# Six raw weight buffers, the decay table moved, first quarters loaded at the release of their home, and another block order

## The chip, the cores and the metric

The kernel runs on one core of one Trainium2 chip. The metric is the device time of one execution in microseconds. The kernel before took 404.04 us, the median of three executions that lie between 403.84 and 404.21 us.

A core has a matrix engine (PE, with the loading of its stationary operand shown as PEld), a vector engine (DVE), an activation engine (ACT), a general engine (POOL) and an engine that here only issues transfers (SP). Each takes its own instructions strictly in the order in which the program lists them and waits on semaphores where it needs a result of another. Transfers are issued by SP and, where they add to what is already there, by POOL.

## The reference

A decoder layer in float32 on x of shape (1, 256, 1024):

```python
h = rms_norm(x, g_pre_mix[l])
proj = h @ w_in[l]
...
mo = merge_heads(moba_attention(mq, mk, split_heads(mv, MOBA_HEADS)))
...
ro = retention(rq, rk, split_heads(rv, RET_HEADS))
ro = ro * lax.rsqrt(jnp.mean(ro * ro, axis=-1, keepdims=True) + NORM_EPS)
ro = jax.nn.silu(rg) * merge_heads(ro).astype(x.dtype)
mix = jnp.concatenate([mo, ro], axis=-1) @ w_out[l]
x = x + rms_norm(mix, g_post_mix[l])
h = rms_norm(x, g_pre_cross[l])
mem_n = rms_norm(mem, g_mem[l])
c = cross_attention(h, mem_n, w_cq[l], w_ckv[l], w_co[l])
x = x + rms_norm(c, g_post_cross[l])
h = rms_norm(x, g_pre_ffn[l])
gu = h @ w_gate_up[l]
f = (jax.nn.silu(gu[..., :D_FF]) * gu[..., D_FF:]) @ w_down[l]
x = x + rms_norm(f, g_post_ffn[l])
```

D_FF is 2816. The retention multiplies its scores by a fixed table, `inner_decay`, which the kernel reads from its constants. The FFN holds about half of the weights, and the change is mainly about it.

## The kernel before

**Arithmetic.** A float32 operand is split in a high part and a low part: ACT copies it to a rounded type (line 193), DVE subtracts that copy from the original (line 194). A product is then three matmuls, high by high, high by low, low by high. All weights come in blocks of 128 x 1024 floats (512 KB), and each block goes the same way: SP loads it to a raw buffer, `split_weight` (line 177) splits it into a tile of 128 x 2 x 1024 from the ring `hl` of nine, and PE uses it.

**Buffers.** The pool `rawp` has `RAW` = 5 raw buffers. Three single tiles named `qv`, `kT` and `ret` (128 x 2048 floats each) hold attention operands at first and serve as "homes" in the FFN. The constants `cst` are one tile of 1600 columns, of which the last 1024 are the decay table (line 117), loaded by `mem_stats` (line 977) and read in `ret_scores` (line 425). The retention's values `rv` fill the first half of the tile `ret` (line 950).

**Steps.** The program is written out by a planner in Python. It makes a list of 259 steps, each some six or eight matmuls; the FFN begins with step 129. The loop over the steps (line 1034) issues the step's matmuls, then whatever side work has come due (`run_side`: evacuations, activations, transposes, whose delays in steps stand in the table `WAIT`), and then at most one split (lines 1145 to 1156). A split is issued when a ring tile will have been free for two steps, and either nothing else was issued in this step or its first use is near (`near`, `now`); `hold` forbids splits around the first steps of the FFN.

**Blocks of the FFN.** The first four of the 22 column tiles go as plain blocks (weights 64 to 71). The names in the lists mean: `r6` is the gate and the up block of column tile 6, taken in rows (four steps); `d3` is block 3 of the down projection (two steps, one for each half of the tokens); `2:5` is product 5 of column group 2 (two steps, one for each of two blocks a and b). The groups 2, 3 and 4 are computed as a fast 2 x 2 block product with seven products in place of eight. `USE` is the order in which PE takes the blocks, `SPLIT` the order in which they are split (and loaded).

**Chains.** Of the seven products of a group, number 2 has a weight block of its own. The weight of number 1 (W11) is loaded to the group's home `one`, that of number 3 (W22) to home `two`; these are the "first quarters". The weights of the others are sums that are made in the home: after a split, POOL issues a transfer that adds another quarter in place (line 202), or DVE adds the other home (line 200, groups 3 and 4). Home `one` serves products 1, 5, 6, 4 in this order, home `two` products 3 and 7. `HOMES` names them: group 2 has kT and qv, group 3 qv and kT, group 4 ret and qv.

**Loading.** `load_weight` (line 140) is called after every split of a plain block and takes the next entry of `queue`, so a block's load is issued after the split of the block five places earlier in the queue. A first quarter is an entry of the same queue: when it comes up, SP is given its load at once and then the next plain block's. SP takes these loads in order. A load to a raw buffer waits until the split that last read the buffer is done, and a load to a home until the last reader of the home is done.

**Evacuating a group.** `seven_done` (line 663): after product 2 DVE adds and ACT applies the SiLU `s_silu` steps later; after product 3 DVE subtracts and multiplies, and `s_t0` steps later PE transposes the first half of the tokens (`f_store`, line 651, the tile `c_f`); after product 4 ACT applies the SiLU (line 682), `s_mul` steps later DVE multiplies (line 684), and `s_t1` steps later PE transposes the second half. The first column tiles go through `ffn_gate` (SiLU, line 587, delay `fg0`) and `ffn_up` (product on DVE, line 578, transposes `f0_0` steps later, line 582).

Of the kernel before, what the change touches and what calls it, by code (L numbers as in the profile page):

```python
# [7 lines left out]
F32 = mybir.dt.float32  # L8
# [3 lines left out]
ALU = mybir.AluOpType  # L12
AX = mybir.AxisListType

P = 128
D = 1024
EPS = 1e-6
MOBA_HEADS = 8
RET_HEADS = 4
CROSS_HEADS = 4  # L20
RING = 9
RAW = 5
FFN_Q = 64
HOMES = {2: ('kT', 'qv', None), 3: ('qv', 'kT', None), 4: ('ret', 'qv', None)}
SEVEN = tuple(HOMES)
ON_CHIP = (3, 4)
USE = 'r6 r7 r4 2:1 r5 r20 d3 d0 r21 2:5 2:6 d2 d1 2:2 d21 2:3 d4 2:7 d5 2:4 3:1 d20 3:2 d8 d7 d9 d6 3:5 3:6 3:3 3:7 d11 3:4 4:1 d10 4:2 4:5 d13 d12 4:6 4:3 d14 4:7 d15 4:4'.split()
SPLIT = 'r6 r4 r7 r5 2:1 r20 d0 d3 r21 2:5 d2 2:2 2:3 2:6 d1 2:7 d21 d4 d5 2:4 3:1 3:2 d8 d7 d20 d6 d9 3:5 3:3 3:6 3:7 d11 4:1 3:4 d10 d13 d12 4:2 4:5 4:3 4:6 d14 4:7 d15 4:4'.split()
DOWN_END = (16, 17, 18, 19)
ROW_TILES = tuple(int(what[1:]) for what in USE if what[0] == "r")  # L30
ROWS_AT = FFN_Q + 8
# [2 lines left out]

WAIT = {
    "cpb0": 2, "cpb1": 1, "cpv0": 7, "cpv1": 1, "cu0": 3, "cu1": 4, "ex_c0": 2, "ex_c1": 1, "ex_m00": 0,
    "ex_m10": 0, "ex_m11": 4, "f0_0": 9, "f0_1": 7, "g_add": 0, "g_silu": 5, "gate0": 3, "gate1": 6,
    "gp1": 5, "gp2": 0, "k_add": 0, "k_hl": 3, "lag": 2, "low": 6, "mq": 0, "mrow": 3, "ms": 21, "mst": 5,
# [5 lines left out]
}  # L44
WARM = 9

# [6 lines left out]
def tile_hybrid_layer(  # L53
# [45 lines left out]
    def accC(name):  # L99
        return psC.tile([P, 4, P], F32, tag="C", name=name)  # L100

    cst = cpool.tile([P, C_END], F32, tag="cst", name="cst")
    xg = cpool.tile([P, 288], F32, tag="xg", name="xg")
    gp = xg[:, 0:32].rearrange("p (g k) -> p g k", g=4)
    x_sb = cpool.tile([P, 2, D], F32, tag="x", name="x_sb")
# [8 lines left out]
    msin = cst[:, C_MSIN:C_MSIN + 32].rearrange("p (t d) -> p t d", t=2)  # L114
    rcos = cst[:, C_RCOS:C_RCOS + 128].rearrange("p (t d) -> p t d", t=2)
    rsin = cst[:, C_RSIN:C_RSIN + 128].rearrange("p (t d) -> p t d", t=2)
    decay = cst[:, C_DEC:C_DEC + 1024].rearrange("p (h i) -> p h i", h=RET_HEADS)

    T = {}
    rstd = {}  # L120
# [16 lines left out]
    queue = []  # L137
    sums = {}

    def load_weight():  # L140

        if not queue:
            return
        q = queue.pop(0)
        kind, w = items[q][:2]
        if kind == "w":
            raws[q] = rawp.tile([P, D], F32, tag="raw", name=f"raw{q}")
            nc.sync.dma_start(raws[q], weights[w])
        else:
            g, home, part = items[q][2:5]  # L150
            if part == 0:
                sums[(g, home)] = actp.tile([P, 2, D], F32, tag=home, name=f"sum_{home}{g}")
            nc.sync.dma_start(sums[(g, home)][:, part, :], weights[w])
            if (g, home, part) in beside:
                home, w = beside[(g, home, part)]
                if part == 0:
                    sums[(g, home)] = actp.tile([P, 2, D], F32, tag=home, name=f"sum_{home}{g}")
                nc.sync.dma_start(sums[(g, home)][:, part, :], weights[w])
            load_weight()

    homes = {}
# [1 line left out]
    split_at = {}  # L163
    ret_kept = [1000, 1000]
    beside = {}

    def free_home(q, i):

        if len(ringed) < RING or last_use[ringed[-RING]] + WAIT["lag"] <= i:
            return "hl"  # L170
        if q >= FFN_Q and ("oT", 7, 1) in emitted:
            for tag in ("qv", "kT", "ret") if q < FFN_Q + 8 else ("ret",) if not ret_kept[0] - 8 < q <= ret_kept[1] else ():
                if tag not in homes or last_use[homes[tag]] + WAIT["lag"] <= i:
                    return tag
        return None

    def split_weight(q, parts=1, home="hl"):
        kind = items[q][0]
        if kind == "w":
            raw = raws.pop(q)  # L180
        else:
            g, tag, part = items[q][2:5]
            raw = sums[(g, tag)][:, part, :]
        if home == "hl":
            ringed.append(q)
            h = hlp.tile([P, 2, D], F32R, tag="hl", name=f"hl{q}")
        else:
            homes[home] = q
            h = actp.tile([P, 2, D], F32R, tag=home, name=f"hl{q}")
        w = D // parts  # L190
        for i in range(parts):
            n = slice(i * w, (i + 1) * w)
            nc.scalar.activation(h[:, 0, n], raw[:, n], AF.Copy)  # L193
            nc.vector.tensor_tensor(out=h[:, 1, n], in0=raw[:, n], in1=h[:, 0, n].bitcast(F32), op=ALU.subtract)  # L194
        hls[q] = h
        split_at[q] = step_no[0]
        if kind != "w":
            plus, more = items[q][5:7]
            if plus is not None:
                nc.vector.tensor_tensor(out=raw, in0=raw, in1=sums[(g, plus)][:, part, :], op=ALU.add)  # L200
            if more is not None:
                nc.gpsimd.dma_start(raw, weights[more], accum_op=ALU.add)
        if kind == "w":
            load_weight()

# [203 lines left out]
    def ret_scores():  # L409

        need("rqk0", "rqk1")
        for kb in range(2):
# [7 lines left out]
            for e in range(2):  # L420
                if kb == 0 or e == 0:
                    buf = tmp2k(f"ra{kb}{e}")
                a = buf[:, kb * e * 256:kb * e * 256 + 2 * n].rearrange("p (j i) -> p j i", j=2)
                T[f"ra{kb}{e}"] = a
                nc.vector.tensor_tensor(out=a, in0=s[e][:, 0:2 * n].rearrange("p (j i) -> p j i", j=2),
                                        in1=decay.rearrange("p (j e) i -> p e j i", e=2)[:, e, :, 0:n], op=ALU.mult)
            if kb == 0:
                yield WAIT["rs"]

# [233 lines left out]
    def seven_done(g, m, acc):  # L663
# [3 lines left out]
        elif m == 2:  # L667
            f = parts[(g, 1)]
            nc.vector.tensor_tensor(out=f, in0=acc, in1=f, op=ALU.add)
            yield WAIT["s_silu"]  # L670
            nc.scalar.activation(f, f, AF.Silu)
        elif m == 3:
            f = parts[(g, 6)]
            nc.vector.tensor_tensor(out=f, in0=acc, in1=f, op=ALU.subtract)
            nc.vector.tensor_tensor(out=f, in0=f, in1=parts[(g, 1)], op=ALU.mult)
# [239 lines left out]
    if kept:  # L915
        ret_kept[:] = kept[0], kept[-1]

    last_use, first_use = {}, {}
    for i, s in enumerate(steps):
        last_use[s[1]] = i  # L920
# [26 lines left out]
    T["kT"] = kr[:, 0:1024].rearrange("p (j m) -> p j m", j=4)  # L947
    T["rqT"] = kr[:, 1024:1536].rearrange("p (j m) -> p j m", j=2)
    T["rkT"] = kr[:, 1536:2048].rearrange("p (j m) -> p j m", j=2)
    T["rv"] = actp.tile([P, 2048], F32, tag="ret", name="rv")[:, 0:1024].rearrange("p (t d) -> p t d", t=2)  # L950
    st_tile("xT", "stA")
    st_tile("mixT", "stB")
    xr = [p4.tile([P, 4, 256], F32, tag="p4", name=f"xr{i}") for i in range(2)]
# [17 lines left out]
    def mem_stats():  # L971
        mn = []
        for t in range(2):
            m = pt4.tile([P, D], F32, tag="pt4", name=f"memn{t}")
            nc.sync.dma_start(m, mem[tok(t), :])
            mn.append(m)
        nc.sync.dma_start(cst[:, C_DEC:], consts[:, C_DEC:])
        spawn(load_gpost(0))
        yield WAIT["mst"]
        for t in range(2):  # L980
# [287 lines left out]
```

## Time and profile before

| what | us |
|---|---|
| median of three executions | 404.04 |
| the profiled execution | 404.05 |
| its span, first to last instruction | 402.2 |
| PE busy in the span | 392.8 |
| DVE busy | 298.5 |
| ACT busy | 253.0 |
| POOL busy | 28.8 |
| splits on DVE from a raw buffer (line 194), 114 of 1192 ns on average | 133.6 |
| the same on ACT (line 193), 114 of 1034 ns on average | 114.6 |

The span is counted from the first to the last instruction of the program; the profiled execution took 1.85 us more than its span. A busy PE is not a PE at its peak, since the ends of matmuls are modelled. Where PE lost time is therefore read from the starts of successive matmuls. The transfers move 83.50 MB at a mean of 208 GB/s; 110 loads of 512 KB go to raw buffers, at a median of 4.6 us from issue to landing, and 20 transfers of 512 KB add to a home, at a median between 6.0 and 6.7 us by home.

### The profile page before, as it was taken

What the parts mean: (1) busy time and instruction counts of PE and PEld (TensorE: products, weight loads), DVE (VectorE), ACT (ScalarE), POOL (GpSimd) and SP (SyncE); (2) the same over time, 40 slices, a digit from 0 to 9 for tenths busy, and PEclk for the clock granted to TensorE, in tenths of its full rate; (3) what the DMA queues carried; (4) which work ended last, traced back from release to release, by engine and by line L of the source; (5) the groups of instructions that cost most, each with busy time, mean ns of one, the idle gap of its engine ahead of it and who ended that gap; (6) DMA issues with size and microseconds to landing.
All of it is one profiled execution on the core that took longest, in us unless ns stands there. A gap on an engine that the chain in (4) does not pass through costs nothing.

```text
span 402.2 us, 5538 instructions
## 1 busy us (share of the span) xinstructions
PE 392.8 (98%) x2005; PEld 327.9 (82%) x2005; DVE 298.5 (74%) x436; ACT 253.0 (63%) x434; POOL 28.8 (7%) x41
## 2 busy tenths in 40 slices
PE   9999999999999999999999999999999899999993
PEld 5887777888888888988888888888888688888782
DVE  4875976685879977586667698887759594985964
ACT  5785973955767856485546956766756546664731
POOL 0010010200011000000010001001201020103000
PEclk9999999999999999999999999999999999999998
DMA  7997745268537575516274577989995979977402
GB/s 275 411 344 237 281 157 209 104 209 275 176 145 244 181 230 177 197 50 212 59 257 156 158 260 229 241 277 222 172 363 108 384 225 191 222 295 143 121 0 104
DMA packets 23787, 83.50 MB, mean 208 GB/s; under 512 B 2640, under 2 KB 2896, under 8 KB 23760
## 3 DMA queue, kind: packets, MB, share of 16 engines
q1 hardware_dynamic: 20736, 72.41, 51.4%
q0 software_dynamic: 2880, 10.49, 15.0%
q8 instruction: 15, 0.25, 0.3%
q10 hardware_dynamic: 144, 0.26, 0.2%
q14 instruction: 12, 0.10, 0.1%
HBM read 82.10 MB, written 1.05 MB: 207 GB/s over the span
## 4 chain that ended last, share of the span: by engine, by line
PE 87%; DVE 3%; issue 3%; DMA 3%; ACT 2%; POOL 1%; DVEq 0%; POOLq 0%; ACTq 0%
PE acc L1098 13%; PE acc L1074 11%; PE acc L1075 11%; PE acc L1076 11%; PE acc L1101 7%; PE x L1134 6%; PE down L1120 4%; PE down L1119 4%; PE down L1121 4%; PE y L1134 4%; PE acc L1062 3%; DMA raw<-in_weights_dram 3%; PE z L1134 2%; DVE hl L194 2%; ACT hl L193 1%
## 5 line engine op out<-in xcount | busy, mean ns | idle before, releaser
L194 DVE TENSOR_TENSOR hl<-raw,hl 128x1024 fp32r<-128x1024 f32 (+1 forms) x114 | 133.6, 1192 | 30.6 <-ACT hl L193 30.4
L193 ACT ACTIVATE hl<-raw 128x1024 fp32r<-128x1024 f32 (+1 forms) x114 | 114.6, 1034 | 3.2 <-DMA raw<-in_weights_dram 3.1
L1074 PE MATMUL acc<-hl,xT 128*128 128x512 f32 x80 | 32.9, 411 | 0.0
L1119 PE MATMUL down<-hl,fT 128*128 128x512 f32 x80 | 31.4, 393 | 0.0
L1076 PE MATMUL acc<-hl,xT 128*128 128x512 f32 x80 | 31.3, 392 | 0.0
L1120 PE MATMUL down<-hl,fT 128*128 128x512 f32 x80 | 31.3, 391 | 0.0
L1075 PE MATMUL acc<-hl,xT 128*128 128x512 f32 x80 | 31.2, 390 | 0.0
L1121 PE MATMUL down<-hl,fT 128*128 128x512 f32 x80 | 31.2, 390 | 0.0
L1098 PE MATMUL acc<-x2T,hl 128*128 128x512 f32 x96 | 23.9, 393 | 0.0
L194 DVE TENSOR_TENSOR hl<-sum_qv,hl 128x1024 fp32r<-128x1024 f32 x16 | 19.3, 1219 | 2.0 <-ACT hl L193 2.0
L1098 PEld LDWEIGHTS acc<-x2T,hl 128*128 128x128 f32 x96 | 17.5, 188 | 3.3
L194 DVE TENSOR_TENSOR hl<-sum_kT,hl 128x1024 fp32r<-128x1024 f32 x12 | 14.5, 1218 | 5.9 <-ACT hl L193 5.9
L1120 PEld LDWEIGHTS down<-hl,fT 128*128 128x128 f32 x80 | 15.0, 188 | 3.4 <-DVE hl L194 0.4
L1076 PEld LDWEIGHTS acc<-hl,xT 128*128 128x128 f32 x80 | 15.0, 188 | 3.3
L1074 PEld LDWEIGHTS acc<-hl,xT 128*128 128x128 f32 x80 | 15.1, 189 | 3.2 <-issue 0.3
L1121 PEld LDWEIGHTS down<-hl,fT 128*128 128x128 f32 x80 | 15.0, 188 | 3.2
L1134 PE MATMUL x<-hl,comb 128*128 128x512 f32 x72 | 17.6, 392 | 0.0
L1119 PEld LDWEIGHTS down<-hl,fT 128*128 128x128 f32 x80 | 15.0, 188 | 3.1
L1134 PE MATMUL y<-hl,comb 128*128 128x512 f32 x72 | 17.3, 389 | 0.0
L1075 PEld LDWEIGHTS acc<-hl,xT 128*128 128x128 f32 x80 | 15.1, 189 | 2.6
L1134 PE MATMUL x<-hl,x2T 128*128 128x512 f32 x72 | 17.0, 389 | 0.0
L193 ACT ACTIVATE hl<-sum_kT 128x1024 fp32r<-128x1024 f32 x12 | 12.5, 1053 | 6.1 <-DMA sum_kT<-in_weights_dram 4.7
(256 smaller groups left out, 867.2 us busy)
## 6 DMA issues: line engine op xcount, KB each, us to landing
raw<-in_weights_dram SPq DMA_DIRECT2D x110, 512.0 KB, 4.6
sum_kT<-in_weights_dram POOLq DMA_DIRECT2D x8, 512.0 KB, 6.2
sum_qv<-in_weights_dram POOLq DMA_DIRECT2D x8, 512.0 KB, 6.0
sum_qv<-in_weights_dram SPq DMA_DIRECT2D x6, 512.0 KB, 5.0
sum_kT<-in_weights_dram SPq DMA_DIRECT2D x4, 512.0 KB, 7.0
sum_ret<-in_weights_dram POOLq DMA_DIRECT2D x4, 512.0 KB, 6.7
gpost<-in_gpost_dram SPq DMA_DIRECT2D x3, 512.0 KB, 4.7
x_sb<-in_x_dram SPq DMA_DIRECT2D x2, 512.0 KB, 6.9
```

Of the source, the lines that this page charges most:

```text
L193: nc.scalar.activation(h[:, 0, n], raw[:, n], AF.Copy)
L194: nc.vector.tensor_tensor(out=h[:, 1, n], in0=raw[:, n], in1=h[:, 0, n].bitcast(F32), op=ALU.subtract)
L1062: nc.tensor.matmul(accs[(c, t)], T["xT"][:, hx, q, tok(t)], h[:, hw, :], start=begin, stop=False)
L1074: nc.tensor.matmul(acc, xh, h[:, 0, kk, :], start=(first and kk == 0), stop=False)
L1075: nc.tensor.matmul(acc, xh, h[:, 1, kk, :], start=False, stop=False)
L1076: nc.tensor.matmul(acc, xl, h[:, 0, kk, :], start=False, stop=(last and kk == 1))
L1098: nc.tensor.matmul(acc, hls[q][:, 0, k * P:(k + 1) * P], T[f"{st}_k"][:, k, :], start=begin, stop=end, skip_group_check=True)
L1101: nc.tensor.matmul(acc[:, 0:256], hls[q][:, 1, k * P:(k + 1) * P], T[st][:, 0, k, :], start=begin, stop=end, skip_group_check=True)
L1119: nc.tensor.matmul(acc, fh, wh, start=first, stop=False, skip_group_check=True)
L1120: nc.tensor.matmul(acc, fh, wl, start=False, stop=False, skip_group_check=True)
L1121: nc.tensor.matmul(acc, fl, wh, start=False, stop=last, skip_group_check=True)
L1134: nc.tensor.matmul(acc, a, h[:, w, kk, :], start=begin and kk == 0 and n == 0, stop=end and n == 2, skip_group_check=True)
```

## The change

There are six raw buffers in place of five. The decay table leaves the constants' tile and goes to the unused second half of the tile that holds the retention's values, which gives back the 4096 bytes of each partition that the sixth buffer takes. Group 4 has kT in place of qv as its home `two`. The first quarters of a group whose home served an earlier group are no longer taken from the queue of loads; SP is given their load right after the split of the last item that reads the home (`released`). The lists `USE` and `SPLIT` are in another order, and 11 delays of `WAIT` differ (`ret` only names an 8 that stood in the code). The work of each engine is otherwise the same: the same matmuls, splits and transfers.

```diff
-RAW = 5
+RAW = 6
 FFN_Q = 64
-HOMES = {2: ('kT', 'qv', None), 3: ('qv', 'kT', None), 4: ('ret', 'qv', None)}
+HOMES = {2: ('kT', 'qv', None), 3: ('qv', 'kT', None), 4: ('ret', 'kT', None)}
 SEVEN = tuple(HOMES)
 ON_CHIP = (3, 4)
-USE = 'r6 r7 r4 2:1 r5 r20 d3 d0 r21 2:5 2:6 d2 d1 2:2 d21 2:3 d4 2:7 d5 2:4 3:1 d20 3:2 d8 d7 d9 d6 3:5 3:6 3:3 3:7 d11 3:4 4:1 d10 4:2 4:5 d13 d12 4:6 4:3 d14 4:7 d15 4:4'.split()
-SPLIT = 'r6 r4 r7 r5 2:1 r20 d0 d3 r21 2:5 d2 2:2 2:3 2:6 d1 2:7 d21 d4 d5 2:4 3:1 3:2 d8 d7 d20 d6 d9 3:5 3:3 3:6 3:7 d11 4:1 3:4 d10 d13 d12 4:2 4:5 4:3 4:6 d14 4:7 d15 4:4'.split()
+HOME_LOADS = "late-sp"
+USE = 'r7 r6 r4 r5 2:1 r20 d0 r21 d3 2:5 2:6 d2 2:2 2:3 d1 d21 2:7 d4 2:4 d5 d20 3:1 d8 3:2 d9 d6 3:5 d7 3:6 3:3 3:7 d11 3:4 4:1 d10 d12 d13 4:5 4:2 4:6 4:3 d14 4:7 d15 4:4'.split()
+SPLIT = 'r6 r4 r7 r5 2:1 d0 r20 r21 2:5 d3 d2 2:2 2:3 2:6 d1 2:7 d21 2:4 d4 d5 3:1 3:2 d20 d8 3:5 d9 d7 d6 3:3 3:6 3:7 d11 4:1 3:4 d12 d10 4:2 d13 4:5 4:3 4:6 d14 4:7 d15 4:4'.split()
...
-    "ex_m10": 0, "ex_m11": 4, "f0_0": 9, "f0_1": 7, "g_add": 0, "g_silu": 5, "gate0": 3, "gate1": 6,
-    "gp1": 5, "gp2": 0, "k_add": 0, "k_hl": 3, "lag": 2, "low": 6, "mq": 0, "mrow": 3, "ms": 21, "mst": 5,
+    "ex_m10": 0, "ex_m11": 4, "f0_0": 3, "f0_1": 7, "g_add": 0, "g_silu": 4, "gate0": 3, "gate1": 6,
+    "gp1": 5, "gp2": 0, "k_add": 0, "k_hl": 3, "lag": 2, "ret": 8, "low": 6, "mq": 0, "mrow": 3, "ms": 21, "mst": 5,
...
-    "sc_c0": 0, "sc_c1": 0, "u0": 4, "u1": 3, "u2": 2, "u_add": 0, "u_mul": 4, "u_hl": 4, "xa_cross0": 0, "xa_cross1": 1,
-    "xa_mix0": 8, "xa_mix1": 4, "near": 12, "now": 4, "sum": 6, "ts": 3, "ts0": 3, "ts1": 5, "s_silu": 4, "s_t0": 2, "s_mul": 2, "s_t1": 1, "xd": 3, "xh_cross0": 1, "xh_cross1": 1, "xh_mix0": 2, "xh_mix1": 2, "xn0": 2, "xn1": 2, "hold0": 1, "hold": 2, "hold_low": 3,
-    "xs": 11, "fg0": 2, "fg1": 0, "xw_cross0": 4, "xw_cross1": 3, "xw_mix0": 4, "xw_mix1": 0,
+    "sc_c0": 0, "sc_c1": 0, "u0": 4, "u1": 3, "u2": 2, "u_add": 0, "u_mul": 2, "u_hl": 1, "xa_cross0": 0, "xa_cross1": 1,
+    "xa_mix0": 8, "xa_mix1": 4, "near": 14, "now": 4, "sum": 5, "ts": 2, "ts0": 3, "ts1": 4, "s_silu": 2, "s_t0": 2, "s_mul": 2, "s_t1": 1, "xd": 3, "xh_cross0": 1, "xh_cross1": 1, "xh_mix0": 2, "xh_mix1": 2, "xn0": 2, "xn1": 2, "hold0": 1, "hold": 3, "hold_low": 3,
+    "xs": 11, "fg0": 4, "fg1": 0, "xw_cross0": 4, "xw_cross1": 3, "xw_mix0": 4, "xw_mix1": 0,
...
-    cst = cpool.tile([P, C_END], F32, tag="cst", name="cst")
+    cst = cpool.tile([P, C_DEC], F32, tag="cst", name="cst")
...
+    def load_home(engine, g, home, part, w):
+
+        if part == 0:
+            sums[(g, home)] = actp.tile([P, 2, D], F32, tag=home, name=f"sum_{home}{g}")
+        engine.dma_start(sums[(g, home)][:, part, :], weights[w])
...
         else:
-            g, home, part = items[q][2:5]
-            if part == 0:
-                sums[(g, home)] = actp.tile([P, 2, D], F32, tag=home, name=f"sum_{home}{g}")
-            nc.sync.dma_start(sums[(g, home)][:, part, :], weights[w])
...
+            for key in firsts[q]:
+                if key[:2] not in follows:
+                    load_home(nc.sync, *key)
             load_weight()
...
             if more is not None:
                 nc.gpsimd.dma_start(raw, weights[more], accum_op=ALU.add)
+            for key in released.get(q, ()):
+                load_home(nc.gpsimd if HOME_LOADS == "late-pool" else nc.sync, *key)
...
-                                        in1=decay.rearrange("p (j e) i -> p e j i", e=2)[:, e, :, 0:n], op=ALU.mult)
+                                        in1=T["decay"].rearrange("p (j e) i -> p e j i", e=2)[:, e, :, 0:n], op=ALU.mult)
...
+    if HOME_LOADS != "early":
+        for home in ("kT", "qv", "ret"):
+            users = [key for key in loads if key[1] == home]
+            for a, b in zip(users, users[1:]):
+                follows[b] = a
+                released.setdefault(last_read[a], []).extend(sorted(loads[b], key=lambda k: k[2]))
...
-    T["rv"] = actp.tile([P, 2048], F32, tag="ret", name="rv")[:, 0:1024].rearrange("p (t d) -> p t d", t=2)
+    rvd = actp.tile([P, 2048], F32, tag="ret", name="rvd")
+    T["rv"] = rvd[:, 0:1024].rearrange("p (t d) -> p t d", t=2)
+    T["decay"] = rvd[:, 1024:2048].rearrange("p (h i) -> p h i", h=RET_HEADS)
...
-        nc.sync.dma_start(cst[:, C_DEC:], consts[:, C_DEC:])
+        nc.sync.dma_start(rvd[:, 1024:2048], consts[:, C_DEC:])
```

More of the change, by code (lines that the diff above doesn't have):

```diff
@@ L116, in tile_hybrid_layer @@
     rsin = cst[:, C_RSIN:C_RSIN + 128].rearrange("p (t d) -> p t d", t=2)
-    decay = cst[:, C_DEC:C_DEC + 1024].rearrange("p (h i) -> p h i", h=RET_HEADS)
     T = {}
@@ L149, in load_weight @@
         else:
-            g, home, part = items[q][2:5]
-            if part == 0:
-                sums[(g, home)] = actp.tile([P, 2, D], F32, tag=home, name=f"sum_{home}{g}")
[L153 to L158, printed above, removed]
+            for key in firsts[q]:
+                if key[:2] not in follows:
+                    load_home(nc.sync, *key)
             load_weight()
@@ L165, in tile_hybrid_layer @@
     beside = {}
+    firsts, follows, released = {}, {}, {}
     def free_home(q, i):
@@ L171, in free_home @@
         if q >= FFN_Q and ("oT", 7, 1) in emitted:
-            for tag in ("qv", "kT", "ret") if q < FFN_Q + 8 else ("ret",) if not ret_kept[0] - 8 < q <= ret_kept[1] else ():
+            for tag in ("qv", "kT", "ret") if q < FFN_Q + 8 else ("ret",) if not ret_kept[0] - WAIT["ret"] < q <= ret_kept[1] else ():
                 if tag not in homes or last_use[homes[tag]] + WAIT["lag"] <= i:
@@ L671, in seven_done @@
             nc.scalar.activation(f, f, AF.Silu)
+            emitted.add(("silu", g))
         elif m == 3:
+            need(("silu", g))
             f = parts[(g, 6)]
@@ L916, in tile_hybrid_layer @@
         ret_kept[:] = kept[0], kept[-1]
+    loads, last_read = {}, {}
+    for q, item in enumerate(items):
+        if item[0] == "w":
+            continue
+        kind, w, g, home, part, plus = item[:6]
+        if kind == "first":
+            firsts[q] = [(g, home, part, w)]
+            if (g, home, part) in beside:
+                firsts[q].append((g, beside[(g, home, part)][0], part, beside[(g, home, part)][1]))
+            for key in firsts[q]:
+                loads.setdefault(key[:2], []).append(key)
+        for h in (home, plus):
+            if h:
+                last_read[(g, h)] = q
+    if HOME_LOADS != "early":
[4 more added lines that the diff above has]
+                released.setdefault(last_read[a], []).extend(sorted(loads[b], key=lambda k: k[2]))
     last_use, first_use = {}, {}
```

## The prediction

> **What bounds the kernel now.** I read the page's busy table and its 40 slices first, then the busy time by stretch, then PE's waits, and then the chain of waits around the only hole.
>
> ```profile
> PE 392.8 (98%) x2005; PEld 327.9 (82%) x2005; DVE 298.5 (74%) x436; ACT 253.0 (63%) x434; POOL 28.8 (7%) x41
> ```
> ```profile
> PE   9999999999999999999999999999999899999993
> ```
> ```profile
> 250.00:310.00 60.00, 60.00 (x298) 50.87 (x297) 47.35 (x65) 39.86 (x59) 7.45 (x9) 1.00 0.87 228
> 310.00:320.00 10.00, 8.32 (x39) 6.66 (x39) 5.68 (x6) 3.83 (x6) 0.00 (x0) 1.00 1.01 353
> 320.00:370.00 50.00, 50.00 (x226) 41.39 (x225) 38.87 (x38) 28.43 (x34) 8.74 (x10) 1.00 0.84 222
> ```
>
> After start, stretch length and length again the columns are the busy time of PE, PEld, DVE, ACT and POOL, then PE's granted clock and the DMA share. PE is the bound: every slice but one reads 9 until the tail, and the one with 8 is at 310 to 320 us, where PE is busy for 8.32 of 10 us. The clock is 1.00 there. The change takes no matmul away, so it can only give back holes. PE's own waits say how many there are:
>
> ```profile
> PE c_f L654 <- DVE sg L684: 1.7, 1, 1.7
> PE warm L942 <- PEq L1258: 0.8, 1, 0.8
> ```
>
> The second longest is at the start, before the first weights. The first is the hole, and the chain of waits follows it back (start, duration, what):
>
> ```profile
> 306.81 1.23 DVE hl L194
> 308.04 0.02 issue
> 308.05 6.82 DMA raw<-in_weights_dram
> ...
> 314.95 1.07 ACT hl L193
> ...
> 316.05 1.23 DVE hl L194
> 317.27 0.61 DVE sg L684
> ```
>
> PE waits to transpose the second token half of group 2. Its product (line 684) stands on DVE behind the split of down block d6, whose raw weights landed only at 314.87, because SP could not issue the load before 308.05: the buffer was held until the split of 3:2a ended. SP's waits and issues confirm it:
>
> ```profile
> SPq L148 <- DVE hl L194: 11.5, 2, 10.2
> ```
> ```profile
> SPq L153 <- DMA sum_qv<-in_weights_dram: 12.5, 1, 12.5
> ```
>
> From 298 to 311 us SP stood 10.2 us at a raw buffer, and from 276 to 292 us 12.5 us at the home of 3:1's first quarters, with the raw loads queued behind.
>
> **What the hole costs.**
>
> ```profile
> 315.95 0.39 PE L1121 MATMUL down<-hl,f 128*128 128x512 f32 x1
> 318.02 0.63 PE L654 MATMUL c_f<-cst,sg 128*128 128x128 f32 x4 [1.68 <-DVE sg L684]
> ```
> ```profile
> 347.74 5.44 PE x L1134 x24
> ```
>
> Undisturbed matmuls start every 5.44 / 24 = 0.227 us, so one step of six is 1.36 us. The two starts above are 2.07 us apart: 2.07 - 0.23 = **1.84 us** lost. A second, small loss is at d14:
>
> ```profile
> 370.00 0.60 ACT L666 ACTIVATE s<-x 128x512 f32<-128x512 f32 x1 [5.15 <-PE x L1134]
> 370.50 1.05 ACT L193 ACTIVATE hl<-raw 128x1024 fp32r<-128x1024 f32 x1
> ```
> ```profile
> 372.53 0.39 PE L1119 MATMUL down<-hl,fT 128*128 128x512 f32 x1
> 372.86 0.50 PE L1120 MATMUL down<-hl,fT 128*128 128x512 f32 x1
> 373.20 0.40 PE L1121 MATMUL down<-hl,fT 128*128 128x512 f32 x1
> ```
>
> Starts 0.33 and 0.34 us apart in place of 0.227 lose 0.22 us: d14's split queued on ACT behind the evacuation of 4:6 (370.00).
>
> **The change part by part.** I walked the rules of lines 1143 to 1156 over the new lists and delays; that gives the step at which each split is issued. PE's steps keep their lengths, so times are counted in steps.
>
> *Six buffers.* One load per split is issued as before, five blocks ahead; what goes is the wait. A load takes the buffer of the block six places back, whose split is always an earlier one. In the new order the split between the SiLU and the product of group 2's second half is that of d8 (SiLU at step 194, d8 at 195, product at 196, transposes at 197). Its load stands on SP behind 3:3's two first quarters, which wait for the split of 2:4b:
>
> ```profile
> 300.93 0.69 DVE L674 TENSOR_TENSOR s<-y,s 128x512 f32<-128x512 f32 x1 [2.48 <-PE y L1134]
> 301.72 0.69 DVE L675 TENSOR_TENSOR s<-s,s 128x512 f32<-128x512 f32 x1
> 302.33 1.22 DVE L194 TENSOR_TENSOR hl<-sum_kT,hl 128x1024 fp32r<-128x1024 f32 x1
> ```
> ```profile
> DMA to landing us min/median/max: 3.4/4.6/10.4
> ```
> ```profile
> 261.27 0.90 SPq L153 DMA_DIRECT2D sum_qv<-in_weights_dram  x2
> ```
>
> PE ends 2:3b some 0.2 us before 300.93, the order on DVE stays, so 2:4b's split ends 2.8 us after 2:3b. Two issues on SP (0.90) bring d8's load to 4.0 us with its own, and a raw load lands 3.4 to 10.4 us later (the row is that of line 148): between 7.4 and 14.4 us. ACT wants it after the SiLU of 2:4, which ends ten steps later: 10 x 1.36, 0.44 of transposes, 0.2 and 0.6 make 14.8 us. Even the slowest load of the trace is in time. Without this cover each microsecond of lateness is one of PE.
>
> *The wait after the data.* SiLU, one split, product, transposes: the same sequence stands in group 3 of before, with the raw weights there in time.
>
> ```profile
> 350.49 0.60 ACT L682 ACTIVATE sg<-x 128x512 f32<-128x512 f32 x1 [1.10 <-PE x L1134]
> ```
> ```profile
> 353.21 0.68 DVE L684 TENSOR_TENSOR sg<-s,sg 128x512 f32<-128x512 f32 x1
> ```
> ```profile
> 354.38 0.60 PE L654 MATMUL c_f<-cst,sg 128*128 128x128 f32 x4
> ```
>
> The product ends at 353.89, the transposes start 0.5 us later without a wait. So the 1.84 us go, with a cover of some 0.5 us.
>
> *d14.* Its split is issued at step 235, ahead of the evacuation at step 236. It then starts at least 0.6 us earlier: 0.22 us go.
>
> *First quarters late.* 3:1's loads wait for 2:7b's split as before; what was queued behind them on SP is now ahead of them. 3:3's no longer wait for their turn in the queue, and 4:3's wait for 3:7b in home kT instead of 3:4b in qv, five steps earlier. Nothing on POOL is moved past a wait: its 20 accumulating transfers come in the order of the splits.
>
> *Decay table.* The same transfer at the same place; the tile's next user is the cross-attention's query, long after. Cost 0; the retention finds the table loaded.
>
> *Order and delays.* No split is issued fewer than four steps (5.4 us) before its use; in the old order d14 had three and 4:6b two. A split needs 1.05 on ACT and 1.23 on DVE, and up to 0.8 behind an evacuation: 3.1 us. The rest, 2.3 us, covers a second split in front (1.2). The tightest new place is the opening of the FFN, below. Before the FFN the order is unchanged and PE has no hole that loads could close, so earlier raw loads bring 0 there.
>
> **Sum.** 404.05 (profiled, span 402.2 and 1.85 around it) - 1.84 - 0.22 = 401.99; the median is 0.01 below the profiled execution, so **402.0 us**. Below it there is no other hole to close; 401.7 leaves room for the spread of the three executions. Above it stand the rivals.
>
> **Rivals.**
>
> *A new wait at the opening* (faster all the same). `f0_0` 9 to 3 asks for the first transposes six steps earlier, `fg0` 2 to 4 for the SiLU two steps later.
>
> ```profile
> 226.53 1.28 ACT L587 ACT_TABLE_LOAD   x1
> 227.83 0.60 ACT L587 ACTIVATE sg<-acc 128x512 f32<-128x512 f32 x1
> 228.32 1.14 ACT L511 ACTIVATE x2T<-xt_cross,xg 128x128 fp32r<-128x128 f32 x4
> ```
> ```profile
> 226.64 0.44 PE xt_cross L508 x4
> ```
>
> After the transposes end (227.08) the new order has on ACT a wait of 0.2, four evacuations (1.14), a split (1.05), the table load (1.28) and the SiLU (0.60), then the product on DVE (0.69, as DVE's operations of that size above): 4.9 us. PE comes to the transposes four steps later, 5.4 us: a cover of 0.5 us. If DVE takes one split (1.22) in front, PE loses 0.7: **402.7 us**.
>
> *The wait comes back elsewhere* (no change). The cover of 0.5 us before group 2's transposes is less than one split: a second one in front of the product on DVE costs 0.7, and data late by 1 us more costs the rest. That the sixth buffer doesn't help because five loads are issued ahead as before belongs here; SP's 10.2 us at the buffer speak against it, since the load's turn had come. **403.2 to 404.5 us.**
>
> *Accumulating transfers get slower* (slower). SP's loads now run further ahead, beside POOL's.
>
> ```profile
> DMA to landing us min/median/max: 5.4/6.1/10.5
> ```
> ```profile
> 328.31 0.88 POOL L202 DMA_DIRECT2D sum_kT<-in_weights_dram  x1 [20.25 <-DVE hl L194]
> ```
>
> The second row is that of line 202; the stretch with the hole has a DMA share of 1.01. The closest chain: 3:3a is split at step 205 and 3:7a, which needs its sum, used at 217: 16.3 us less one step (1.36) for step 205 itself is 15.0. The split behind an addition of group 3 takes 0.2 + 0.69 + 1.23, the issue 0.2 + 0.88, then the landing, and 3:7a's own split 2.3: 5.5 us and the landing, so 9.5 us of landing are covered. The median leaves 3.4 us, the slowest (10.5) costs 1.0. Slower than before by over 0.2% needs 2.06 + 0.81 = 2.9 us: landings near 12.4 us at one place, or 10.5 at three of the chains' pairs. Priced at 11.2 at each of two pairs: 2 x 1.7 = 3.4, **405.4 us**. Against it: the same number of bytes moves, and loads that start earlier are also done earlier.
>
> The Trainium skill ("DMA: Bandwidth & Descriptors", "Issuing engines are not separate DMA queues") says the same thing against the change: transfers started by different engines run on the same 16 DMA engines and interleave. The stretch's DMA share agrees that there is no room at such moments; by that rule this rival's time would come out, by the landings of the trace the forecast. The page's fit for a transfer ("Anatomy of one DMA", 2.0 us and the bytes over 436 GB/s) would give an estimate of 3.2 us for 512 KB and no such rival at all; the trace's median of 6.1 us is what decides.
>
> **How the numbers follow.** Chances: the forecast with up to 0.6 us of small new waits (401.7 to 402.6) 0.60; a new wait at the opening or like it (402.6 to 403.2) 0.10; the wait back elsewhere 0.17; slower 0.13. Some 0.2% (0.8 us) is what a measurement of this kernel can tell from no change, so faster means under 403.23, slower over 404.85: 0.70, 0.17, 0.13. The range takes in the first two and most of the third, 401.7 to 404.0.
>
> **What would show it.** Right: in the stretch of the second transposes of group 2 PE is busy throughout, the row of `c_f` behind `sg` is gone from PE's waits, SP no longer stands 10 us at a raw buffer there, and d14's matmuls start 0.227 us apart. Wrong: a wait of `c_f` behind `f` or `sg` (first and second rival), or of PE behind `hl` with ACT waiting for an accumulating transfer (third).

## The result and the profile after

The changed kernel took 401.37 us, the median of four executions between 401.11 and 401.58 us. The kernel before took 404.02 us in the same comparison (four executions, 403.84 to 404.21). The ratio is 0.9934, with a 95% interval from 0.9917 to 0.9951. The forecast was 402.0 us in a range from 401.7 to 404.0: the direction was right, and the time lies 0.33 us below the range's lower end. The profiled execution after took 401.58 us and its span is 399.8.

The page of the changed kernel, its busy times and PE's 40 slices:

```profile
PE 392.3 (98%) x2005; PEld 328.0 (82%) x2005; DVE 299.8 (75%) x436; ACT 254.3 (64%) x434; POOL 28.7 (7%) x41
...
PE   9999999999999999999999999999999999999993
```

The work is the same, 2005 matmuls among it, and the slice that read 8 now reads 9. The busy time by stretch, in the columns used before (start, length twice, PE, PEld, DVE, ACT, POOL, PE's clock, DMA share, GB/s):

```profile
250.00:310.00 60.00, 60.00 (x297) 50.83 (x297) 47.44 (x62) 39.09 (x58) 6.98 (x8) 1.00 0.90 242
310.00:320.00 10.00, 10.00 (x48) 8.29 (x47) 6.99 (x7) 6.47 (x8) 0.00 (x0) 1.00 0.99 340
320.00:370.00 50.00, 50.00 (x226) 41.37 (x226) 38.53 (x38) 29.49 (x35) 8.72 (x10) 1.00 0.81 207
```

In the middle row PE was busy for 8.32 us with 39 matmuls, now for 10.00 with 48. PE's waits in the whole execution (waited in total, times, longest) are down to two, and neither is in the FFN:

```profile
PE warm L968 <- PEq L1286: 0.8, 1, 0.8
PE c_R_mem L246 <- POOL r_mem L217: 0.2, 1, 0.2
```

The place of the old hole, in the timeline of PE and then of DVE (start, duration, what). The transposes of group 2's second half start 0.24 us after the last matmul ahead of them; it was 2.07 us.

```profile
313.01 0.40 PE L1149 MATMUL down<-hl,f 128*128 128x512 f32 x1
313.25 0.60 PE L657 MATMUL c_f<-cst,sg 128*128 128x128 f32 x4
```

```profile
310.94 1.23 DVE L195 TENSOR_TENSOR hl<-raw,hl 128x1024 fp32r<-128x1024 f32 x1 [1.79 <-ACT hl L194]
312.08 0.68 DVE L689 TENSOR_TENSOR sg<-s,sg 128x512 f32<-128x512 f32 x1
```

The product ends at 312.76, so the transposes have a cover of 0.5 us, as forecast. The split in front of it is now that of d8, whose load had been issued by 299.20 and landed at 304.16, 5.7 us before ACT took it at 309.85. SP's waits from 298 to 311 us:

```profile
SPq L154 <- DVE hl L195: 7.5, 4, 4.1
```

The longest wait at a raw buffer fell from 10.2 to 4.1 us. At d14 the matmuls start 0.23 and 0.22 us apart, which were 0.33 and 0.34:

```profile
370.44 0.39 PE L1147 MATMUL down<-hl,fT 128*128 128x512 f32 x1
370.67 0.39 PE L1148 MATMUL down<-hl,fT 128*128 128x512 f32 x1
370.89 0.39 PE L1149 MATMUL down<-hl,fT 128*128 128x512 f32 x1
```

**A measure that leaves the start out.** From here on the starts of the matmuls are used in two parts: "48th" is the start of the 48th matmul of the first weights (line 1062 before, 1090 after), and "rest" the time from there to the start of PE's last matmul. What remains of a profiled execution behind and around them is 8.75 us before and 8.64 after, and between 8.6 and 9.2 in all 14 profiles of this study.

| profile | 48th | rest | its time |
|---|---|---|---|
| before | 16.59 | 378.71 | 404.05 |
| after | 16.37 | 376.57 | 401.58 |

The rest fell by 2.14 us, where the forecast said 1.84 + 0.22 = 2.06. The profiled times differ by 2.47: 2.14, 0.22 by which this start came sooner, and 0.11 around.

### The profile page after: what moved, and what is told of

It reads as the page before. It is cut to its first block, busy times and chain, and to the rows that moved or that the text cites. A ratio compares the mean times of both kernels' runs of the same rounds, so it can differ in the third digit from the quotient of the medians.

```text
span 399.8 us, 5537 instructions
## 1 busy us (share of the span) xinstructions
PE 392.3 (98%) x2005; PEld 328.0 (82%) x2005; DVE 299.8 (75%) x436; ACT 254.3 (64%) x434; POOL 28.7 (7%) x41
## 4 chain that ended last, share of the span: by engine, by line
PE 92%; DVE 3%; issue 2%; ACT 1%; POOL 1%; DVEq 0%; POOLq 0%; ACTq 0%
PE acc L1126 13%; PE acc L1102 11%; PE acc L1103 11%; PE acc L1104 11%; PE x L1162 8%; PE acc L1129 7%; PE down L1147 5%; PE down L1149 4%; PE down L1148 4%; PE y L1162 4%; PE acc L1090 3%; PE z L1162 2%; PE warm L968 1%; DVE hl L195 1%; ACT p_m L310 1%
## 5 line engine op out<-in xcount | busy, mean ns | idle before, releaser
L195 DVE TENSOR_TENSOR hl<-sum_kT,hl 128x1024 fp32r<-128x1024 f32 x16 | 19.5, 1221 | 8.3 <-ACT hl L194 8.3
L194 ACT ACTIVATE hl<-sum_kT 128x1024 fp32r<-128x1024 f32 x16 | 16.7, 1053 | 2.3 <-DMA sum_kT<-in_weights_dram 2.3
L1126 PE MATMUL acc<-memT,hl 128*128 128x512 f32 x64 | 16.3, 396 | 0.0
```

What stands on the lines that cost most here:

```text
L1126: nc.tensor.matmul(acc, hls[q][:, 0, k * P:(k + 1) * P], T[f"{st}_k"][:, k, :], start=begin, stop=end, skip_group_check=True)
```

## The experiments

Two questions were open. Which part closes the hole: the sixth buffer, the new order, or the late first quarters? And why is the time lower than the sum allowed: is there a further gain (for one, that a sixth buffer lets SP load further ahead from the first weights on, so that PE starts sooner), or was the kernel before profiled in an execution that started late? All kernels were timed in five rounds, beside the kernel before on the same chip. That one had medians of 403.64 (14 executions), 403.36 (23) and 403.48 us (9) there, and lay anywhere from 402.87 to 405.02.

### The parts one by one

The changed kernel again, unedited:

> The changed kernel once more, unchanged, to size the gain with more rounds. Theory A (only the two holes of the FFN are closed, 1.84 + 0.22 us, and the rest of the measured 2.65 us is scatter of the executions): 2.0 to 2.2 us under the kernel before, ratio 0.9945 to 0.9950, and the first weight matmul starts as often near 4.99 us as near 4.89 us. Theory B (the sixth buffer or the new place of the tiles also starts the kernel sooner): 2.4 to 2.8 us under it, ratio 0.993 to 0.994, and the excess of the first ten microseconds stays near 1.08 us where before had 1.30 us.

Measured: 401.25 us (six executions, 400.76 to 401.69), ratio 0.9938 [0.9922, 0.9954]. The rest is 376.59, 0.02 from the first profile; the 48th matmul starts at 15.75, 0.62 us sooner. One kernel, two starts. By its time it lies where theory B put it, 2.39 us under the kernel before; by its rest, 2.12 us under that of before, it lies with theory A.

Buffers alone: six raw buffers and the table moved to make room, with the old order and the old way of loading (the diff is against the kernel after).

```diff
-HOMES = {2: ('kT', 'qv', None), 3: ('qv', 'kT', None), 4: ('ret', 'kT', None)}
+HOMES = {2: ('kT', 'qv', None), 3: ('qv', 'kT', None), 4: ('ret', 'qv', None)}
-HOME_LOADS = "late-sp"
+HOME_LOADS = "early"
...
-USE = 'r7 r6 r4 r5 2:1 r20 d0 r21 d3 ...
+USE = 'r6 r7 r4 2:1 r5 r20 d3 d0 r21 ...
...
```

> The kernel before with six raw buffers and the decay table in the retention's tile; old order, delays and homes, first quarters still taken from the queue. Theory A: the load of d6 is issued near 298 us in place of 308 us, the hole of 1.84 us at group 2's second transposes goes, the 0.22 us at d14 stay: 402.2 us, ratio 0.9955. Theory B: 0.3 to 0.6 us less, 401.6 to 401.9 us. Theory C (the order of the blocks is what closes the hole, and buffers don't): near 404.0 us, with the wait of c_f behind sg kept.

Measured: 401.92 us (401.40 to 402.70), 0.9955 [0.9939, 0.9972]; the rest is 376.88, that is 1.83 below before. PE's timeline at the old hole:

```profile
315.78 0.40 PE L1149 MATMUL down<-hl,f 128*128 128x512 f32 x1
316.02 0.60 PE L657 MATMUL c_f<-cst,sg 128*128 128x128 f32 x4
```

The hole is gone, since d6's load no longer waits for 3:2a's split: it landed at 304.41. The ratio is the one that theory A gave. The loss at d14 stays, 0.22 of the 0.31 us that it has more than the kernel after.

The order alone: five buffers and the old way of loading, with the new lists and delays.

```diff
-RAW = 6
+RAW = 5
...
-HOME_LOADS = "late-sp"
+HOME_LOADS = "early"
```

> The changed kernel with five raw buffers and the first quarters taken from the queue as before; new order, delays and homes, table moved. Theory A (as refined here: either a sixth buffer or the new order is enough, since in the new order the split in front of the product is that of d8, whose buffer d4 gives back near step 189, so that the load has some 5 steps before it is wanted): no wait of c_f, d14 closed too, 402.0 us, ratio 0.995. Theory C: the same 402.0 us. A theory in which the buffers alone do it: the hole of 1.84 us is still there, 403.8 us.

Measured: 401.44 us (nine executions, 400.88 to 403.11), 0.9950 [0.9933, 0.9966]; the rest is 377.15. This closes the hole too, but leaves a small new loss. SP's issues in its timeline (x4 are four loads), and PE's timeline 37 us later:

```profile
302.13 7.11 SPq L154 DMA_DIRECT2D raw<-in_weights_dram  x4
309.34 1.37 SPq L144 DMA_DIRECT2D sum_kT<-in_weights_dram  x2
```

```profile
346.33 0.39 PE L1149 MATMUL down<-hl,fT 128*128 128x512 f32 x1
346.80 0.70 PE L1162 MATMUL x<-hl,x2T 128*128 128x512 f32 x2
```

3:3's first quarters come only after loads that stand at raw buffers, so the sum of 3:7 is late; the two starts are 0.47 apart in place of 0.227, 0.24 us, and 0.19 more go at 343 us. In the kernel after SP issues these two loads at 297.92.

The late first quarters alone: five buffers, the old lists, delays and home, and `HOME_LOADS = "late-sp"`.

```diff
-RAW = 6
+RAW = 5
...
-USE = 'r7 r6 r4 r5 2:1 r20 d0 r21 d3 ...
+USE = 'r6 r7 r4 2:1 r5 r20 d3 d0 r21 ...
...
```

> The kernel before with the first quarters loaded at the release of their home, five raw buffers, old order, delays and homes, table moved. Theory A: d6 still waits for the buffer of 3:2a (issue near 308 us), its load lands 1 us sooner at best since fewer transfers are under way, and the hole keeps 0.8 to 1.84 us: 403.0 to 404.0 us. A rival, that SP blocked by 3:1's first quarters was the cause of the late load: hole gone, 402.2 us.

Measured: 406.45 us, the median of five executions between 405.57 and 407.24 (a sixth took 802.27, which nothing here explains, and is left out); 1.0067 [1.0047, 1.0086]: **slower than before**, which neither of the two forecasts had. The rest is 381.24, 2.53 us more than before. The chain of waits has the hole of before, with a slower load:

```profile
307.16 7.80 DMA raw<-in_weights_dram
...
315.04 1.07 ACT hl L194
...
316.13 1.23 DVE hl L195
317.36 0.61 DVE sg L689
```

This execution started 0.90 us sooner (its 48th at 15.69), so the load was issued at the same point of the work as in before (308.05 there). It took 7.80 us in place of 6.82, and PE's hole is 3.04 - 0.23 = 2.81 us in place of 1.84: the delay passes straight through. Then comes a second loss. PE's timeline, and the stretch by busy time:

```profile
315.06 0.39 PE L1149 MATMUL down<-hl,f 128*128 128x512 f32 x1
318.10 1.09 PE L657 MATMUL c_f<-cst,sg 128*128 128x128 f32 x4 [2.66 <-DVE sg L689]
...
319.41 0.63 PE L1148 MATMUL down<-hl,f 128*128 128x512 f32 x1
319.84 0.63 PE L1149 MATMUL down<-hl,f 128*128 128x512 f32 x1
```

```profile
318.00:321.00 3.00, 2.90 (x9) 2.54 (x10) 0.89 (x2) 1.77 (x3) 0.00 (x0) 0.50 1.03 414
```

Behind the hole the granted clock is 0.50 and the matmuls start 0.43 us apart in place of 0.227. The trace's record of the clock says half speed for 3.413 us, from 317.91 to 321.32. That is what remains, 2.53 - 0.97 = 1.56 us.

### The parts with one turned back

The change with five buffers:

```diff
-RAW = 6
+RAW = 5
```

> The changed kernel with five raw buffers in place of six. Theory A (each of the two, sixth buffer and new order, closes the hole by itself; late first quarters do no harm where the split in front of the product isn't late): no wait of c_f, PE needs 376.6 us from the 48th matmul of the first weights to its last one, as in the changed kernel, about 2.1 us under the kernel before (ratio 0.995) and what is left of the difference is the start. Rival (late first quarters with five buffers make the load late, as they did in the old order): a hole of 1 to 3 us near 313 us, 403 to 405 us.

Measured: 401.80 us (401.11 to 402.58), 0.9954 [0.9936, 0.9972]; the rest is 376.59.

The change with the old way of loading:

```diff
-HOME_LOADS = "late-sp"
+HOME_LOADS = "early"
```

> The changed kernel with the first quarters taken from the queue of loads again (six buffers, new order). Theory A: the hole stays closed; the 0.6 us that PE lost near 343 and 346 us with five buffers came from 3:3's quarters that were issued only at 309 us behind a raw buffer; with six they are issued some 4 us earlier: loss under 0.2 us, 376.6 to 376.8 us from the 48th matmul to the last, ratio 0.994 to 0.995. Rival (late loading is needed by the new order whatever the buffers): the 0.6 us stay, 377.2 us.

Measured: 401.79 us (400.72 to 402.39), 0.9950 [0.9931, 0.9968]; the rest is 376.61. In the new order either of the two is enough: PE's work behind the start is the same to 0.04 us with both, with the sixth buffer alone, and with the late loading alone.

The change with the old order (six buffers, late loading, old lists, delays and home):

```diff
-USE = 'r7 r6 r4 r5 2:1 r20 d0 r21 d3 ...
+USE = 'r6 r7 r4 2:1 r5 r20 d3 d0 r21 ...
...
```

> Six raw buffers and late first quarters in the old order with the old delays and homes. Theory A: d6 takes the buffer of d5, issued near 298 us, so the hole and the slow clock after it go; d14's 0.22 us stay: 376.85 us from the 48th matmul to the last, ratio 0.9955. Rival (the late quarters of 3:3 delay d6's load whatever the buffers): a hole of 1 us or more near 315 us.

Measured: 402.46 us (twelve executions, 401.69 to 403.44), 0.9970 [0.9957, 0.9982]; the rest is 378.58, as in before. The main expectation missed: in the profiled execution the hole is back, 1.70 us long.

```profile
314.97 0.39 PE L1149 MATMUL down<-hl,f 128*128 128x512 f32 x1
316.89 0.63 PE L657 MATMUL c_f<-cst,sg 128*128 128x128 f32 x4 [1.53 <-DVE sg L689]
```

SP's waits from 290 to 312 us, and the chain:

```profile
SPq L144 <- DVE hl L195: 11.0, 2, 9.0
```

```profile
301.35 1.23 DVE hl L195
...
302.60 0.33 SPq L144
...
302.98 0.42 SPq L144
...
303.44 10.30 DMA raw<-in_weights_dram
...
313.83 1.07 ACT hl L194
...
314.92 1.23 DVE hl L195
316.15 0.61 DVE sg L689
```

SP stands 9.0 us at line 144, the loads of 3:3's first quarters, until 2:4b's split at 301.35 is done. d6's raw load is queued behind them, is issued at 303.44 and takes 10.30 us, where the median of such loads in this trace is 5.1. A raw buffer was free. So two things make this hole: the place in SP's queue, which left 8.5 us until ACT wanted the block (its SiLU ends at 311.92), and a slow transfer. The forecast had priced this very wait for the new order, where 2:4b is split three steps earlier and the split behind the SiLU is d8's: there the load had 5.7 us to spare.

The profiled execution took 403.09 us and was the second slowest of the twelve. The earliest 48th matmul of the 14 profiles (15.60), this rest and the least that remains around it in any of them (8.64) make 402.82 us, and nine of the twelve executions were faster than that. In them the hole must have been shorter or absent, which fits a load whose landing decides.

The decay table alone: before, with the table moved.

```diff
-        nc.sync.dma_start(cst[:, C_DEC:], consts[:, C_DEC:])
+        nc.sync.dma_start(rvd[:, 1024:2048], consts[:, C_DEC:])
```

> The kernel before with only the decay table moved to the retention's tile. Theory A: no difference, 378.7 us from the 48th matmul to the last, hole of about 1.84 us, ratio 1.000 within 0.2%. Theory B (places in memory or six buffers start the kernel sooner): the 48th matmul comes earlier than the 16.59 us of the kernel before only in kernels with the new place; here then by 0.2 us or more and the time by as much under the kernel before.

Measured: 403.56 us (twelve executions, 402.98 to 404.93), 1.0004 [0.9992, 1.0016]; the rest is 378.59. It costs nothing. The 48th matmul starts at 15.85, 0.74 us sooner than in the profile of before, but the time isn't lower, and a start at 17.21 came with the new place too: nothing speaks for theory B.

All eight combinations of order, buffers and loading are now there; "order" stands for the lists, the delays and group 4's home together, which no run takes apart. The rest in us, of one profile each:

| | early, 5 buffers | early, 6 | late, 5 | late, 6 |
|---|---|---|---|---|
| old order | 378.71 | 376.88 | 381.24 | 378.58 |
| new order | 377.15 | 376.61 | 376.59 | 376.57 |

Two of these are not the rest of every execution: 378.58, as said above, and 377.15, since three of nine executions (400.88 to 401.21) lie under 15.60 + 377.15 + 8.64 = 401.39 us.

### The start

The 14 profiles start their 48th matmul between 15.60 and 17.21 us, at a median of 15.82. Of the ten up to here, with that of before and the first after, five have six buffers and a mean of 16.19 (16.37, 15.75, 16.38, 16.82, 15.62), and five have five buffers and a mean of 16.19 too (16.59, 17.21, 15.69, 15.60, 15.85). So these profiles show no sooner start with the sixth buffer; a few tenths of a microsecond could hide in their scatter. What varies is seen in the chains of the first 20 us: before, after, the change with five buffers, and the change with early loading, of which the first pieces of the start are left in.

```profile
4.99 11.99 PE acc L1062 x48
```

```profile
4.89 11.86 PE acc L1090 x48
```

```profile
4.75 11.24 PE acc L1090 x48
```

```profile
2.10 5.55 DMA xr<-in_gx_dram
7.65 0.02 issue
7.67 0.51 ACT xT L227
8.18 0.53 ACT hl L194
8.71 0.04 issue
8.75 8.46 PE acc L1090 x36
```

The 48 first matmuls take 11.99, 11.86 and 11.24 us for the same work. In the profiles of before and after the second, third and fourth start 0.43 to 0.57 us after the one ahead, the pace of half the clock as in the stretch quoted above; in that with five buffers all are at 0.22 to 0.31. The clock column of the table by stretch reads 1.00 at the start in all of them, so there it doesn't show this. The trace's own record of the clock does. Its first entry, full speed, stands at 6.78 us in before, at 6.36 in after, and at 3.81 with five buffers. In the 14 profiles it stands at 5.40 to 6.78 us in the four whose first weight matmuls run at half pace, and at 3.50 to 4.26 us, ahead of the first weight matmul (4.6 to 5.0), in the ten others.

In the last chain a slice of x landed at 7.65 us, and PE had to wait for it behind matmul 12:

```profile
PE acc L1090 <- ACT hl L194: 1.2, 1, 1.2
```

The late start with the buffers alone (16.38) has neither cause. There a weight block landed at 10.33 us (9.2 to 9.7 in the profiles without a late landing), and its split held PE:

```profile
3.52 6.81 DMA raw<-in_weights_dram
...
10.35 0.64 ACT hl L194
```

Three edits of the start were tried, beside the changed kernel once more.

> The changed kernel a third time, for the comparison on this chip. Theory A: 376.6 us from the 48th matmul of the first weights to PE's last; the 48th itself anywhere between 15.6 and 17.2 us, as in the ten profiles so far, whatever the number of buffers; 2.1 us under the kernel before, give or take the scatter of the start, ratio 0.994 to 0.996. Theory B (the sixth buffer starts the kernel sooner): the 48th at 16.0 us or earlier and the ratio at 0.993 to 0.994.

Measured: 401.00 us (400.79 to 401.47), 0.9943 [0.9931, 0.9956]; the 48th at 15.89, the rest 376.61.

The load of x's second slice ahead of that of half a weight block:

```diff
-        nc.sync.dma_start(raws[1][:, 0:512], ...)
-        nc.sync.dma_start(xr[0][:, 1, :], ...)
+        nc.sync.dma_start(xr[0][:, 1, :], ...)
+        nc.sync.dma_start(raws[1][:, 0:512], ...)
```

> The changed kernel with the small load of x's second slice issued ahead of the first half of raw block 1. Theory A (the start scatters because in some executions that slice lands 1.4 us late, as in two of ten profiles, and in others the matmul clock is still at half for the first matmuls): the late landing is gone or rare, the 48th matmul at 15.6 to 16.6 us, spans of the six executions between 398.9 and 399.9 us, median 0 to 0.3 us under the changed kernel's. Rival (the slice's place among the transfers doesn't matter): the same spread as the changed kernel, 0 difference.

Measured: 400.91 us (400.81 to 401.61), 0.9944 [0.9932, 0.9957]; 48th 15.63, rest 376.57.

That half weight block issued by ACT:

```diff
-        nc.sync.dma_start(raws[1][:, 0:512], ...)
+        nc.scalar.dma_start(raws[1][:, 0:512], ...)
```

> The changed kernel with the first half of raw block 1 issued by ACT right behind its first load, ahead of its table load, in place of SP, so that each later load of SP is issued 0.47 us earlier. If the start is bound by the order of issue: the slice of x and block 1 land 0.3 to 0.5 us earlier, the 48th matmul at 15.6 to 16.2 us, median 0.2 to 0.4 us under the changed kernel's. If it is bound by the rate at which the first transfers come in: the first weight block itself lands later, 0 to 0.3 us slower.

Measured: 401.47 us (401.12 to 401.60), 0.9952 [0.9939, 0.9964]; 48th 15.77, rest 376.57.

A tenth matmul that only keeps PE busy before the first weights:

```diff
-WARM = 9
+WARM = 10
```

> The changed kernel with ten in place of nine matmuls on constants ahead of the first weights. If the half clock of the first weight matmuls (0.43 us apart in place of 0.227, in three of ten profiles) comes from too little matmul activity before them, it is gone, median 0 to 0.3 us less; if not, the tenth ends near 4.6 us, ahead of the first weights in most executions, and costs 0 to 0.2 us.

Measured: 401.60 us (401.05 to 401.72), 0.9956 [0.9943, 0.9970]; 48th 15.80, rest 376.61.

None of the three can be told from the changed kernel, which has 15.75, 15.89 and 16.37 as its own starts and 400.76 to 401.69 us as the times of its 15 executions, and no version beats it beyond its scatter. The gain of 0.2 to 0.4 us forecast for the load issued by ACT did not come.

## Why the prediction came out as it did

**Six buffers, and the wait after the data: right.** The 1.84 us went entirely, by the path that was forecast: the load's turn at SP came earlier, the split was ready when ACT came to it, and the product ended 0.5 us before PE wanted it. The rival that five loads issued ahead leave nothing for a sixth buffer fell with the buffers alone (376.88). Where the forecast was too narrow is in naming the buffer as what closes the hole: the new order with five buffers and late loading reaches 376.59 as well.

**First quarters late: right for the new order, and for a reason that mattered.** They were let pass because d8's load still had time. In the old order the same edit brings the hole back in the profiled execution (six buffers, 378.58) or makes it larger (five, 381.24). The cover that the forecast worked out is what the order provides.

**d14: right.** 0.22 us forecast; the matmuls now start 0.23 and 0.22 us apart, so it went.

**Decay table: right**, 1.0004 with an interval on both sides of 1.

**The new wait at the opening: did not come.** The opening's product in DVE's timeline and its transposes in PE's:

```profile
230.86 0.69 DVE L581 TENSOR_TENSOR f<-acc,sg 128x512 f32<-128x512 f32 x1 [0.60 <-ACT sg L590]
```

```profile
232.11 0.60 PE L585 MATMUL c_f<-cst,f 128*128 128x128 f32 x4
```

The product ends at 231.55 and PE comes to the transposes 0.56 us later, without a wait. The cover worked out was 0.5 us. (The terms listed for it add up to 4.96 us, not 4.9; the cover of 5.44 - 4.96 = 0.48 is the same.)

**Accumulating transfers: slower, but covered.** The landings of line 203 after the change, whose minimum, median and maximum follow, agree with the rule of the Trainium skill ("DMA: Bandwidth & Descriptors", "Issuing engines are not separate DMA queues") that transfers of different engines share the 16 DMA engines, though no run here takes sharing apart from other causes:

```profile
DMA to landing us min/median/max: 5.5/7.1/10.1
```

against 5.4, 6.1 and 10.5 before. The median rose by 1.0 us (by 1.4 in the two further profiles of the changed kernel); 9.5 us were covered at the closest chain, and PE waits for none. The forecast's reason was loads that run further ahead. The runs point elsewhere: with the buffers alone the median is 6.3, with the late loading alone it is 7.4.

**The step that failed is the sum's anchor and its lower bound.** It read "Below it there is no other hole to close; 401.7 leaves room for the spread of the three executions". Its terms were nearly right: 2.06 us forecast, 2.14 measured. But it took them from one profiled execution at 404.05, beside a median of three (404.04), as if that were the kernel's time to 0.3 us, and so put the scatter of the start at nothing. That execution's 48th matmul started at 16.59, 0.77 us later than the median of the 14 profiles. The same sum from a typical start is 404.05 - 0.77 - 2.14 = 401.1 us, and the medians of the changed kernel were 401.37, 401.25 and 401.00. Of the 0.62 us between 401.99 and 401.37, the size of the terms makes 0.08, the sooner start of the profile after 0.22, what remains around it 0.11, and the median of the four executions lies 0.21 below the profiled one. The prediction had the sign in hand: it named PE's second longest wait as the one before the first weights, and said that loads could close no hole before the FFN. It didn't ask whether the start repeats. Three executions within 0.4 us did not show that it does: over the 46 others, before ranged over 2.15 us, with medians 0.4 to 0.7 us under 404.04.

What stays open: the medians of the changed kernel lie 2.4 to 2.65 us below those of before, 0.25 to 0.5 more than the 2.14 of the profiles. In the first comparison, with the largest gain, the four executions of before had a median of 404.02, as the anchor had it; whether all four started late isn't on record. The fastest executions of the two kernels differ by 2.11 us (402.87 and 400.76), which points to the slower ones of before for the excess. The hole of before is set by when one load lands, so it can be longer in executions that weren't profiled. One bears a sign of it: the slowest of the 46 (405.02) has a mean granted clock of 0.991, as the executions with the late quarters alone have (0.989 to 0.991), whose profile shows half clock behind the hole; the other 45 have 0.994 to 0.999. But five or six executions of a kernel can also be off by as much: the changes with five buffers and with early loading have the same rest as the changed kernel, and 0.4 to 0.8 us more by their medians. The runs don't separate these. Nor do they settle why a slice of x or a weight block lands late in one execution and not in the next.

## What to carry to other kernels

A buffer, an order and a load's place in a queue are three ways to move one load earlier: where a wait ends on a transfer, look for what the issuing engine was standing at, and count a load that you delay as a delay of everything queued behind it. An edit can be free in one order and cost 2.5 us in another, so undo each part in both. And before a forecast within a few tenths of a per cent is hung on one profile, ask of its start, apart from the rest, how far it repeats: here the part behind the start held to 0.04 us in three profiles of the changed kernel, and the start alone moved by 1.6 over all profiles.

## What was not expected of the hardware

**A hole of 3.04 us halved PE's clock; three of 1.92 to 2.07 did not.** These are the distances of the two starts around the hole: the first with the late quarters alone, the others in before, with the table moved, and with six buffers and late loading in the old order. The half clock lasted 3.413 us by the trace's record and cost 1.56 us, over half as much as the hole itself. In that record full speed lasts 23, 92, 114, 115 or 116 times 3.4133 us from one change to the next in all 14 profiles, so the clock changed at the ends of stretches of this length only. With the late quarters alone PE stood still for 2.6 us of the one stretch that ended at 317.91; in the three others for at most 1.7 us of one, and in before the end of a stretch (317.40) falls inside the hole, as it does with the table moved (316.02). So where a hole lies in these stretches may matter as well as its length; four holes don't give the bound. The Trainium skill ("TensorE: Matmul & The Clock Gate", Part 1) states a window of 3413 ns that runs free of the program, and half rate after about one idle window; the length agrees to the nanosecond, but here a gap shorter than one window was enough.

**The start of the same program is not the same.** The 48th matmul came between 15.60 and 17.21 us. Three things are seen. In four of 14 profiles the first weight matmuls run at half pace, which costs 0.3 to 0.8 us though nine matmuls keep PE busy ahead of them; there the clock record has full speed only from 5.40 to 6.78 us on. In two a slice of x landed at 7.65 and 8.04 us in place of 5.9 to 6.6, and PE waited 1.2 us. In one a weight block landed at 10.33 us. The same part of the Trainium skill says that with a free-running window one kernel meets a different number of slow matmuls from run to run; the four profiles agree.
